# Accumulating the last product of a quad on the bank of the fifth, and setting the output scalings one step further back

## The chip, the cores and the metric

The kernel runs on one core of one Trainium2 chip. The metric is the device time of one execution in microseconds; a version's time is the median of its runs. The engines are named as in the profile: PE is TensorE (matmuls; PEld its weight loads), DVE is VectorE, ACT is ScalarE, POOL is GpSimd, and SP is SyncE, which issues the DMAs.

## The reference

One layer of a gated mixer over 2048 tokens of width 1024, in float32:

```python
h = rms_norm(x, g_pre) * (1 + scale) + shift          # scale, shift, gate from c
pv, pg, hq, hf, hi, hg, mg_pool, mg_hgrn = split(h @ w_in)
pooled = multiscale_pool(pv) @ pool_w * pool_scale
branch_a = (pooled * silu(pg)) @ w_pool_o
f = lb + (1 - lb) * sigmoid(hf);  k = 1 - f;  q = silu(hq)
o = rms_norm(hgrn2(q, k, hi, log(f)), hgrn_norm_g)    # 8 heads of 128
branch_b = (o * silu(hg)) @ w_hgrn_o
merged = sigmoid(mg_pool) * branch_a + sigmoid(mg_hgrn) * branch_b
x = x + gate * rms_norm(merged @ w_out, g_post)
```

hgrn2 is a gated linear recurrence with a 128x128 state for each head. The norm of its output `o` needs, for each token, the sum of squares over the head's 128 channels.

## The kernel before

The tokens are done in two passes of 1024, each as two tiles of 512 tokens (t = 0 and 1). In a pass, the value projection comes first (`psV`), then the eight heads, then the two branches' output projections (`psA`, `psB`), then the output projection (`psy`, in the second pass `ray` and `rxy`).

**Quads.** In the heads, the input projection is done by `quad` (line 522). A quad multiplies a pair of column blocks of `w_in` with both token tiles, a 2x2 block product, by seven products instead of eight (a Strassen-Winograd scheme). Each of the seven is twelve matmuls of 128x512 by `three` (line 327): four blocks of the inner dimension, and for each high x high, high x low and low x high halves of the numbers; all matmuls are issued by line 325. The seven are called by their right-hand side, in this order: `B11`, `T1`, `T2`, `B21`, `T3`, `B22`, `T4`. They accumulate in PSUM banks from a pool of four (`bank`, line 338): `a` (in the profile `pafq`, `pagp`, `pam`, by the kind of quad), `b` (`pb..`), `e` (`pe..`) and `d` (`pd..`). `B11` starts `a`, which is copied to `b`; `T1` starts `e`, copied to SBUF as `s5` (`c22..` in the profile); `T2` adds to `a`, copied out as `u2` (`c12..`); `B21` adds to `b`, the first output; `T3` adds to `a`; `B22` adds to `e`; `T4` adds to `d`. The copies out of PSUM are on ACT (lines 531, 536 and 549), the additions `tt(s5, a, s5)` and `tt(u2, e, u2)` on DVE (line 443, the helper `tt`). Each head has three quads: fq (forget gate and query), m (the two merge gates) and gp (output gate and a pool block); heads 0 to 6 run them in the order fq, m, gp and head 7 in the order fq, gp, m. That makes 48 quads over both passes. The function `got` passes an output on: to a sigmoid on ACT and, for all but the m quads and the forget gate, a multiplication on DVE.

**Steps.** The recurrence of a head (`hgrn`, line 575, one generator for each t) is interleaved with the quads: six times in a quad, and once after it, `tick` advances every active generator by one `yield`. The recurrence of head h starts after its fq quad. Its score matmuls (`psa`) use GAP = 5 steps between levels; DVE puts the scores into a triangle (`PT`, lines 625 and 631) and multiplies K and Q by decays; ACT copies blocks of Q into `X` (lines 658, 661 and 691). In its 25th step, which falls after the fourth product of the next head's second quad, PE makes the output `po`, ACT squares it and sums (`junk`, line 740), POOL turns the sums `ss` into reciprocal roots (line 741, and line 443 with `pow`). In the step after, ACT scales the output by `ss` into `on` (line 746, four for each t). Two steps later PE transposes it (`pot`, line 751), DVE multiplies it by the gate (line 753), and `two_out` splits it into high and low parts and stores both by two DMAs on SP (`Gd`).

**Order.** The source gives the order of the steps, but the order of the instructions in an engine's queue is planned when the program is built: among the instructions that are expected to be ready, the older goes first, and a tile gets its buffer from its pool when one is free. Most tiles of 128x512 share one pool of 76 buffers (`utile`). Weights are read four products ahead (`take`, `prep`), split into high and low parts by ACT and DVE (`whl`, line 173), and in the second pass read back ready split.

Of the kernel before, what the change touches and what calls it, by code (L numbers as in the profile page):

```python
# [70 lines left out]
def tile_block(ctx: ExitStack, tc: tile.TileContext, x, c, w_ada, b_ada, g_pre, g_post, w_in,  # L71
# [3 lines left out]
    V, A, G, PE, SP = nc.vector, nc.scalar, nc.gpsimd, nc.tensor, nc.sync  # L75
# [16 lines left out]
    def utile(name, dt=F32):  # L92
        return up.tile([P, T], dt, tag="u", name=name)
# [219 lines left out]
    def take(look=LOOK):  # L313
        if outs:
            store("out", *outs.pop(0))
        i = state["use"]
        state["use"] = i + 1
        while len(ready) < i + look and more():
            prep()
        w = ready[i]  # L320
        ready[i] = None
        return w[:, 0:T], w[:, T:2 * T]
# [4 lines left out]
    def three(ps, w, rhs, start, stop):  # L327

        hi, lo = w
        n = len(rhs)  # L330
        for k in range(n):
            wh, wl = hi[:, k * P:(k + 1) * P], lo[:, k * P:(k + 1) * P]
            rh, rl = rhs[k]
            mm(ps, wh, rh, start and k == 0, False)
            mm(ps, wh, rl, False, False)
            mm(ps, wl, rh, False, stop and k == n - 1)

    def bank(name):
        return pj.tile([P, T], F32, tag="pj", name=name)
# [96 lines left out]
    def v2(ap, n):  # L436
        return ap.rearrange("p (a b) -> p a b", b=n)
# [4 lines left out]
    def tt(o, a, b, op=MUL, e=None):  # L442
        return (e or V).tensor_tensor(o, a, b, op=op)  # L443
# [78 lines left out]
    def quad(name, cx, got, tick):  # L522

        mv = cx["mv"]

        def prod(ps, nm, start):
            three(ps, take(), [mv[nm, i] for i in range(4)], start, True)

        def snap(ps, nm):
            o = utile(f"{nm}{name}")  # L530
            A.copy(o, ps)
            return o

        a, b = bank("pa" + name), bank("pb" + name)
        prod(a, "B11", True)
        A.copy(b, a)
        e = bank("pe" + name)
        prod(e, "T1", True)
        s5 = snap(e, "c22")
        tick()  # L540
        prod(a, "T2", False)
        u2 = snap(a, "c12")
        tick()
        prod(b, "B21", False)
        got(0, 0, b)
        tick()
        d = bank("pd" + name)
        prod(a, "T3", False)
        A.copy(d, a)
        tt(s5, a, s5, op=ADD)  # L550
        got(1, 1, s5)
        tick()
        prod(e, "B22", False)
        tt(u2, e, u2, op=ADD)
        got(0, 1, u2)
        tick()
        prod(d, "T4", False)
        got(1, 0, d)
        tick()


# [13 lines left out]
    def hgrn(p, h, t, cx):  # L575
# [13 lines left out]
        for hh in (1, 2, 4, 8, 16, 32, 64):  # L589
            w = T // (2 * hh)  # L590
            a = v2(Tb[hh], 2)
# [129 lines left out]
        pd = px.tile([P, NT, P], F32, tag="px", name="pd" + n)  # L721
# [18 lines left out]
            A.activation(junk[:, 0:P], po[:, cc, :], AF.Square, accum_out=ss[:, cc:cc + 1])  # L740
        G.tensor_scalar(ss, ss, 1.0 / P, EPS, op0=MUL, op1=ADD)
        tt(ss, ss, mh[:, 0:NT], op=ALU.pow, e=G)
        yield
        on = utile("on" + n)
        for cc in range(NT):
# [394 lines left out]
    def tick():  # L1140
        for g in list(active):
            try:
                next(g)
            except StopIteration:
                active.remove(g)
# [38 lines left out]
    for p in range(NPASS):  # L1184
# [65 lines left out]
        for h in range(NH):  # L1250
# [19 lines left out]
            def tick_in():  # L1270
                htick()
                once(steps)

            quad("fq" + n, cx, fq, htick)
            active.extend(hgrn(p, h, t, cx) for t in range(2))
            htick()
            for i, kind in enumerate(KINDS[h == NH - 1]):
                if kind == "gp":
                    quad("gp" + n, cx, gp, htick)
                else:  # L1280
                    if h == NH - 1:
                        steps += [lambda: None] * 2
                        steps += [lambda g=g: two_in("P", p, g, cx) for g in range(NG - 1)]
                    quad("m" + n, cx, lambda row, t, u: m_got(p, h, row, t, u, cx), tick_in)
                htick()
# [63 lines left out]
```

## Time and profile before

| | |
|---|---|
| time before, median of 3 runs | 1829.64 us (1827.5 to 1830.42) |
| the profiled execution, its own time | 1831.51 us |
| its span, first to last instruction | 1829.7 us |
| mean granted TensorE clock | 0.996 |
| 140 to 1045 us, from the first quads to those of the second pass | PE busy 891.34 of 905.00 us |
| second pass up to the end of the heads, 1045 to 1600 us | PE busy 550.39 of 555.00 us |

A line of the waits gives who waited, for whom, the microseconds in total, how many times, and the longest. A line of a timeline gives the start and the duration in microseconds, engine, line, operation, output<-inputs, shapes, count, and in brackets the idle time before it with what ended it. A line of the chain of waits gives start, duration and what the chain consists of there. A line for a tile gives minimum, median and maximum in nanoseconds.

### The profile page before, as it was taken

How to read it: one execution, taken by the hardware profiler on the slowest of the kernel's cores; microseconds unless marked ns; L12 is line 12 of the kernel's file. 1: busy time of each engine (PE TensorE's matmuls, PEld its weight loads, DVE VectorE, ACT ScalarE, POOL GpSimd, SP SyncE). 2: the span in 40 equal slices, each digit the busy share in tenths (PEclk: the TensorE clock that was granted, in tenths of full speed). 3: DMA queues.
4: the chain of work that ended last, by engine and by line, in shares of the span. 5: the costliest groups of instructions: out<-in, count | busy, mean ns of one | idle time of the engine just before them, and what ended most of it. 6: DMA issues, size and time to landing. Idle time of an engine off the chain costs nothing.

```text
span 1829.7 us, 32049 instructions
## 1 busy us (share of the span) xinstructions
PE 1772.8 (97%) x12005; PEld 1449.7 (79%) x12005; DVE 1148.9 (63%) x2460; ACT 826.9 (45%) x1939; POOL 77.6 (4%) x136
## 2 busy tenths in 40 slices
PE   5899999999999999999999999999999999999997
PEld 4788878788788787887788878888788788888885
DVE  7577887787888884565443266566566555623446
ACT  4655656556666572223322345455455354310032
POOL 1100000000000100000000000000000000000001
PEclk9999999999999999999999999999999999999998
DMA  8698676777767669987887776876876755695457
GB/s 301 207 321 289 219 271 231 253 253 242 259 236 255 238 222 320 353 304 258 303 293 255 267 256 208 288 259 212 285 238 215 237 179 189 202 348 190 137 208 275
DMA packets 255540, 460.98 MB, mean 252 GB/s; under 512 B 20077, under 2 KB 129306, under 8 KB 255386
## 3 DMA queue, kind: packets, MB, share of 16 engines
q1 hardware_dynamic: 255386, 458.95, 73.1%
q8 instruction: 94, 1.54, 0.3%
q14 instruction: 60, 0.49, 0.1%
HBM read 271.70 MB, written 187.17 MB: 251 GB/s over the span
## 4 chain that ended last, share of the span: by engine, by line
PE 79%; ACT 5%; DMA 4%; DVE 4%; POOL 2%; issue 2%; SPq 0%; POOLq 0%; DVEq 0%; ACTq 0%
PE psB L325 9%; PE psV L325 8%; PE pagp L325 7%; PE pafq L325 7%; PE pam L325 5%; PE pefq L325 5%; PE psA L325 4%; PE pegp L325 4%; PE psy L325 3%; PE pem L325 3%; PE psa L325 3%; PE pbfq L325 2%; PE pdfq L325 2%; PE pdm L325 2%; PE pbm L325 2%; PE pbgp L325 2%
## 5 line engine op out<-in xcount | busy, mean ns | idle before, releaser
L173 DVE TENSOR_TENSOR whl<-wr,whl 128x512 fp32r<-128x512 f32 x210 | 144.1, 690 | 85.7 <-ACT whl L173 84.4
L173 ACT CAST whl<-wr 128x512 fp32r<-128x512 f32 x210 | 130.0, 620 | 127.7 <-PE psB L325 26.5
L325 PE MATMUL psV<-whl,hB 128*128 128x512 f32 x512 | 162.6, 400 | 1.4 <-ACT V L840 1.4
L325 PE MATMUL psB<-Gh,whl 128*128 128x512 f32 x512 | 158.6, 390 | 0.0
L325 PEld LDWEIGHTS psV<-whl,hB 128*128 128x128 f32 x512 | 97.7, 193 | 21.5 <-ACT V L840 1.7
L631 DVE COPY_PREDICATED PT<-mask,psa 128x256 f32<-128x256 uint8 x160 | 86.2, 548 | 44.3 <-PE psa L325 44.2
L325 PEld LDWEIGHTS psB<-Gh,whl 128*128 128x128 f32 x512 | 96.1, 188 | 20.4 <-issue 0.5
L325 PE MATMUL psV<-whl,lB 128*128 128x512 f32 x256 | 101.2, 397 | 0.0
L325 PE MATMUL psB<-Gl,whl 128*128 128x512 f32 x256 | 100.0, 391 | 0.0
L325 PE MATMUL pam<-hT,whl 128*128 128x512 f32 x256 | 87.4, 402 | 0.0
L325 PE MATMUL pagp<-hT,whl 128*128 128x512 f32 x256 | 86.2, 397 | 0.0
L325 PE MATMUL psA<-Ph,whl 128*128 128x512 f32 x256 | 82.6, 397 | 3.4 <-DMA Ph<-Pd 1.7
L325 PE MATMUL pafq<-hT,whl 128*128 128x512 f32 x256 | 84.0, 389 | 0.0
L443 DVE TENSOR_TENSOR K<-K,TT 128x256 f32<-128x256 f32 x192 | 81.4, 425 | 0.7 <-PE psa L325 0.7
L325 PE MATMUL psy<-whl,mgh 128*128 128x512 f32 x256 | 80.6, 395 | 0.7 <-DVE y L443 0.7
L325 PEld LDWEIGHTS psa<-X,K 128*32 128x32 f32 x2816 | 50.0, 110 | 30.0 <-issue 19.2
L325 PE MATMUL psa<-X,K 128*32 128x48 f32 (+2 forms) x2816 | 60.7, 208 | 2.7 <-DVE PT L625 2.7
L443 DVE TENSOR_TENSOR sm<-psB,sm 128x512 f32<-128x512 f32 x32 | 22.0, 688 | 63.8 <-PE psB L325 62.4
L625 DVE COPY_PREDICATED PT<-mask,psa 128x256 f32<-128x256 uint8 (+1 forms) x96 | 52.0, 542 | 12.0 <-PE psa L325 11.9
L325 PEld LDWEIGHTS psA<-Ph,whl 128*128 128x128 f32 x256 | 47.6, 188 | 15.0 <-DMA Ph<-Pd 3.5
L325 PEld LDWEIGHTS psV<-whl,lB 128*128 128x128 f32 x256 | 49.1, 192 | 10.5
L325 PEld LDWEIGHTS pagp<-hT,whl 128*128 128x128 f32 x256 | 48.0, 188 | 10.9 <-issue 0.2
(437 smaller groups left out, 4532.2 us busy)
## 6 DMA issues: line engine op xcount, KB each, us to landing
wr<-in_w_in_dram SPq DMA_DIRECT2D x122, 256.0 KB, 4.7
whl<-scr_y SPq DMA_DIRECT2D x44, 512.0 KB, 4.7
sm<-Sd SPq DMA_DIRECT2D x64, 256.0 KB, 4.6
whl<-scr_v SPq DMA_DIRECT2D x32, 512.0 KB, 4.2
scr_y<-rfy SPq DMA_DIRECT2D x56, 256.0 KB, 3.2
wa<-in_w_ada_dram SPq DMA_DIRECT2D x32, 256.0 KB, 5.4
x<-in_x_dram SPq DMA_DIRECT2D x32, 256.0 KB, 5.4
Vd<-V SPq DMA_DIRECT2D x32, 256.0 KB, 2.4
```

Of the source, the lines that this page charges most:

```text
L173: return A.copy(hi, src32), V.tensor_tensor(lo, src32, hi.bitcast(F32), op=SUB)
L325: PE.matmul(o, lhsT=l, rhs=r, start=start, stop=stop, skip_group_check=True)
L443: return (e or V).tensor_tensor(o, a, b, op=op)
L625: V.copy_predicated(dst.rearrange("p (c a) b -> p c a b", c=NT), m.unsqueeze(1).broadcast_to(shp), src.unsqueeze(2).broadcast_to(shp))
L631: V.copy_predicated(dst.rearrange("p (c q) a b -> p c q a b", c=NT), m, src.rearrange("p c (a b) -> p c a b", b=b).unsqueeze(2) .broadcast ...
```

## The change

`T4` no longer has a bank of its own. It adds to `a`, after `tt(s5, a, s5)` has read from it what `T3` completed, and the last output is read from `a`. The bank `d` and its copy go, so a quad takes three banks of the pool in place of four. In `hgrn`, a second `yield` stands between the sums of squares and the scalings, so that the scalings and everything behind them in that generator come one step later.

```diff
@@ quad @@
         prod(b, "B21", False)
         got(0, 0, b)
         tick()
-        d = bank("pd" + name)
         prod(a, "T3", False)
-        A.copy(d, a)
         tt(s5, a, s5, op=ADD)
         got(1, 1, s5)
         tick()
@@ quad @@
         tt(u2, e, u2, op=ADD)
         got(0, 1, u2)
         tick()
-        prod(d, "T4", False)
-        got(1, 0, d)
+        prod(a, "T4", False)
+        got(1, 0, a)
         tick()
@@ hgrn @@
         G.tensor_scalar(ss, ss, 1.0 / P, EPS, op0=MUL, op1=ADD)
         tt(ss, ss, mh[:, 0:NT], op=ALU.pow, e=G)
         yield
+        yield
         on = utile("on" + n)
```

## The prediction

> **What bounds the kernel now.** I read the page first (span, busy shares, the chain by engine), then the waits of TensorE, then the chain of waits inside one of the places they name, then the engines' queues there.
>
> ```profile
> span 1829.7 us, 32049 instructions
> ...
> PE 1772.8 (97%) x12005; PEld 1449.7 (79%) x12005; DVE 1148.9 (63%) x2460; ACT 826.9 (45%) x1939; POOL 77.6 (4%) x136
> ...
> PE 79%; ACT 5%; DMA 4%; DVE 4%; POOL 2%; issue 2%; SPq 0%; POOLq 0%; DVEq 0%; ACTq 0%
> ```
>
> TensorE (PE) is busy for 97% of the span, so a change pays only where PE stands still. But 5% of the chain that ended last lies on ACT and 2% on POOL, which is itself busy for 4%: somewhere PE hangs on them. The waits of PE say where (total us, times, longest):
>
> ```profile
> PE psa L385 <- DVE acc L378: 13.4, 4, 9.3
> PE pdm L325 <- ACT pdm L549: 6.9, 12, 0.9
> ...
> PE psa L325 <- DVE PT L625: 2.7, 3, 1.4
> ```
>
> The first is the start of the kernel, which the change does not touch. The second is the line that the change deletes: the last product of an m quad (`T4`, into `pdm`) waits for the copy on line 549, in 12 of the 16 m quads. The fq and gp quads do not appear: there the copy is always done in time. The twelve fit the source: the squares of a head are taken during the next head's second quad, after its fourth product. That is an m quad for heads 1 to 6, six times in each pass; head 0 has no such work, and head 7 runs gp second. The chain of waits in one of them (start, us, what):
>
> ```profile
> 235.34 1.08 POOL ss L443
> ...
> 238.47 1.02 POOL ss L443
> ...
> 239.52 1.14 ACT on L746 x4
> 240.66 0.29 ACT X L658
> 240.96 0.50 ACT pdm L549
> 241.45 0.04 issue
> 241.50 3.04 PE pdm L325 x12
> ```
>
> POOL raises the sums of squares to a power (1.0 us each); ACT's scalings (`on`, line 746) stand in ACT's queue ahead of the copy and wait for that; the copy comes last, and PE after it.
>
> **The change part by part.** *What the twelve waits cost.*
>
> ```profile
> 238.16 0.39 PE L325 MATMUL pem<-hB,whl 128*128 128x512 f32 x1
> ...
> 240.65 0.39 PE L325 MATMUL pem<-hB,whl 128*128 128x512 f32 x1
> 241.50 0.50 PE L325 MATMUL pdm<-hT,whl 128*128 128x512 f32 x1 [0.46 <-ACT pdm L549]
> 241.83 0.40 PE L325 MATMUL pdm<-lT,whl 128*128 128x512 f32 x1
> ```
>
> These are the first and last matmul of the sixth product, then the first two of the last. The pitch is (240.65 - 238.16) / 11 = 0.23 us. `T4` starts 0.85 us after its predecessor, not 0.23: 0.62 lost, and the step after it is 0.33, another 0.10. So 0.72 us are lost where 0.46 are idle: 0.26 beyond the idle time. For all twelve: 6.9 + 12 x 0.26 = 10.0 us, and since PE runs back to back afterwards, nearly all of it reaches the end. That is the whole gain to be had from the copy's going.
>
> *What takes the copy's place.* `T4` now adds to the bank `a` that the addition `tt(s5, a, s5)` on DVE reads, and must wait for that read. The order in the trace is not the source's: each engine's queue was planned ahead, older instructions first among those expected to be ready. So the question is where `c22m`, that addition, stands in DVE's queue.
>
> ```profile
> 238.69 0.43 DVE L443 TENSOR_TENSOR sq<-X,TT 128x256 f32<-128x256 f32 x1
> 240.99 0.42 DVE L443 TENSOR_TENSOR sq<-sq,TT 128x256 f32<-128x256 f32 x1 [1.87 <-ACT X L658]
> 241.45 0.42 DVE L443 TENSOR_TENSOR X<-sq,TT 128x256 f32<-128x256 f32 x1
> 241.79 0.69 DVE L443 TENSOR_TENSOR c22m<-pam,c22m 128x512 f32<-128x512 f32 x1
> ```
>
> The two operations ahead of `c22m` belong to a later step than it, so by plan it was not yet ready. Why not, when the fifth product (`T3`) is over once the sixth has begun at 238.16? The copy reads the same bank first:
>
> ```profile
> L549 ACT COPY pdm<-pam x16: 570/612/616, 167.2 to 1591.5; 128x512 f32<-128x512 f32 x16
> ...
> DVE c22fq L443 <- ACT pdfq L549: 13.6, 13, 1.4
> ```
>
> In 13 of 16 fq quads DVE stands idle until the copy has ended and only then adds, though both read the same finished bank: the two reads run one after the other. Without the copy the addition is ready some 0.6 us sooner by plan. Does that lift it over the two others? ACT's queue bounds when the plan had the fifth product end:
>
> ```profile
> 240.53 0.42 ACT L658 COPY X<-sq 128x256 f32<-128x256 f32 x1
> 240.83 0.61 ACT L549 COPY pdm<-pam 128x512 f32<-128x512 f32 x1
> ...
> 241.86 0.43 ACT L661 COPY X<-sq 128x256 f32<-128x256 f32 x1
> ```
>
> Line 658's copy is younger in the source than the bank copy and yet goes first, so by plan the product ended after it was issued. Line 661's, which needs the DVE operation fed by 658, goes later, so the product ended before that operation had run. The end lies in a stretch of about 0.3 us of ACT plus 0.35 of DVE. In its first half DVE is still free and takes `c22m` first; in its second half `c22m` follows one operation. The second pass is alike:
>
> ```profile
> 1139.78 0.43 DVE L443 TENSOR_TENSOR X<-sq,TT 128x256 f32<-128x256 f32 x1
> 1141.62 0.42 DVE L443 TENSOR_TENSOR sq<-sq,TT 128x256 f32<-128x256 f32 x1 [1.41 <-ACT X L691]
> 1141.96 0.42 DVE L443 TENSOR_TENSOR sq<-X,TT 128x256 f32<-128x256 f32 x1
> 1142.41 0.69 DVE L443 TENSOR_TENSOR c22m<-pam,c22m 128x512 f32<-128x512 f32 x1
> ...
> 1143.02 0.42 DVE L443 TENSOR_TENSOR X<-sq,TT 128x256 f32<-128x256 f32 x1
> ```
>
> Here `c22m` overtakes the younger operation at 1143.02 which could have run before it. It was ready by plan at about the end of the one at 1141.96. Less the copy's 0.6, that is when the one at 1141.62 was issued, or before. I take it that `c22m` moves ahead of the operations that wait for ACT. It then runs at about 239.1 to 239.8 in the first case, in DVE's idle 1.87 us, against 240.88 when `T4` is due (240.65 + 0.23): 1.1 us in hand. In the second it ends by 1140.9, 1.5 us before the copy did, where no wait of the twelve was over 0.9. So the term is -10.0 us; the other end is the first rival.
>
> *The other 36 quads* have no wait now. `T4` stays covered by the sixth product as long as the addition ends in time. The latest I found:
>
> ```profile
> 262.83 0.69 DVE L443 TENSOR_TENSOR c22gp<-pagp,c22gp 128x512 f32<-128x512 f32 x1
> ...
> 263.06 0.39 PE L325 MATMUL pdgp<-hT,whl 128*128 128x512 f32 x1
> ```
>
> It ends 0.46 us after `T4` started. One or two such cases: +0.5 us, at most 1.
>
> *The bank* `a` is now held until the last output is read. The next quad's first copy may need that bank only after a product of 12 matmuls; the reader it waits for is short:
>
> ```profile
> L443 DVE TENSOR_TENSOR sq<-pdfq,sq x16: 690/692/693, 153.2 to 1549.8; 128x512 f32<-128x512 f32 x16
> ...
> 245.41 2.75 PE pagp L325 x12
> ```
>
> A sigmoid and this multiplication, some 1.4 us, against 2.75: nothing. Three banks a quad out of four leave one spare; the cost would be the difference if readers fell behind by more than 1.4 us. ACT loses 48 copies (x 0.5 = 24 us), but apart from those twelve waits PE hangs on no ACT copy here: nothing.
>
> *The scalings.* One more empty step moves 8 scalings on ACT, then 8 transposes on PE, two multiplications, the splits and four stores on SP by one step. The transposes stay right after `T4`, since no product lies between the two steps; the stores are read back only after all heads. In an m quad no new buffer of the common pool is asked for between the old place and the new, and nothing older is ready for ACT until the fifth product ends. So I expect the same place in ACT's queue, and the wait for POOL to stay:
>
> ```profile
> ACT on L746 <- POOL ss L443: 27.3, 26, 1.4
> ```
>
> It may move in head 7:
>
> ```profile
> 673.50 0.63 ACT L803 ACTIVATE sgg<-c22gp 128x512 f32<-128x512 f32 x1 [0.19 <-DVE c22gp L443]
> 674.04 2.16 ACT L746 ACTIVATE on<-po,ss 128x128 f32<-128x128 f32 x8
> ```
>
> The scalings already stand behind the output before them, which asks for a buffer; they would go behind the next output, some 2.5 us later, and PE can run a product first. Between 0 and +1 us for each of two; I take 0. Should the scalings move in the m quads too, ACT and DVE are free sooner and the term of 10.0 stays as it is.
>
> Sum: -10.0 + 0.5 = -9.5 us. The profiled execution took 1831.5 us (span 1829.7 and 1.8 around it), so 1822.0 for it; it lies 1.9 above the median of 1829.6, which gives 1820.1.
>
> **The rivals.** *First, slower: the addition stays behind the operations that wait for ACT.* Then `T4` waits for the end of `c22m` (241.79 + 0.69 = 242.48) where it waited for the copy's (240.83 + 0.61 = 241.44): +1.04 us. In the second pass the copy ended about when `c22m` starts, 1142.41, and +0.69 follows. Together 6 x 1.04 + 6 x 0.69 = +10.4 us, with the 0.5 of the gp quads +10.9: 1840.5. For it: that is today's order. Against it: today's order comes from the copy. It decides from the point where `c22m` ends more than 0.6 us after its slot.
> [...]
>
> *Second, no change: half and half.* If `c22m` comes after one operation (240.99, the next starts 0.34 later), it ends at 241.33 + 0.69 = 242.02, 0.58 after the copy's end. First in one pass and second in the other: -6 x 0.72 + 6 x 0.58 + 0.5 = -0.3 us: 1829.3.
>
> *Third, no change: the scalings go so late that the transposes wait.* Eight take 2.16 us (row above). If they start only when `T4` is nearly done, the transposes can begin on the first four, and PE waits for the other half: 12 x 1.08 = 13.0 against the 10.0 gained, with the 0.5 +3.5 us: 1833.1.
>
> **How the numbers follow.** The forecast has 0.58: the argument on the order rests on two bounds that agree, but on no row that shows it. The first rival has 0.20, the second 0.14, the third 0.08. About 0.2%, 3.7 us, is what a measurement can tell here. Faster 0.58, same 0.22, slower 0.20. Low end: 1829.6 - 10.0 - 2.7 (the `psa` waits for DVE, which is relieved too) = 1816.9, so 1816. High end: the cases of no change, the dearer at 1833.1, so 1834; the slower rival, 0.20, is left out.
>
> **What would show it.** Right: no row of PE `pam` waiting for `c22m`; `c22m` starting within 1.2 us of the fifth product's end in the twelve m quads; ACT with 48 copies fewer; `on` still waiting for POOL. Wrong: PE waits of 1 us or more on `c22m` (first rival), waits on some and not on others (second), PE `pot` waiting for `on` (third). If no such wait is there and the time has not fallen, PE lost it elsewhere, and I have missed what.

## The result and the profile after

The changed kernel took 1817.22 us (median of 7 runs, 1815.48 to 1823.29) against 1829.64 (7 runs, 1826.39 to 1832.3): a ratio of 0.9936, interval 0.9925 to 0.9947, so 12.4 us less, 9.7 to 13.7 by the interval. Forecast were 9.5 us. In a later comparison, on another chip, the same change gave 1818.95 against 1830.35, ratio 0.9936 [0.9924, 0.9948]. The profiled execution took 1819.84 us.

The page of the changed kernel: span, busy time, and the chain by engine.

```profile
span 1818.1 us, 32014 instructions
...
PE 1769.1 (97%) x12005; PEld 1449.7 (80%) x12005; DVE 1148.2 (63%) x2460; ACT 799.7 (44%) x1891; POOL 77.3 (4%) x136
...
PE 86%; DMA 5%; DVE 2%; ACT 1%; issue 1%; POOL 1%; SPq 0%; POOLq 0%; DVEq 0%; ACTq 0%
```

ACT has 48 instructions fewer and lost 27 us of work, which is not why the kernel is faster (the experiments show it). What matters is the last row: ACT and POOL, 7% of the chain before, are 2% now.

TensorE's waits (us in total, times, longest) of the changed kernel:

```profile
PE psa L385 <- DVE acc L378: 13.0, 4, 9.7
...
PE pam L325 <- DVE c22m L443: 1.2, 1, 1.2
...
PE pagp L325 <- ACT PV L762: 0.7, 1, 0.7
...
PE pagp L325 <- DMA whl<-scr_('gp', 1)_4_2641: 0.4, 1, 0.4
PE pagp L325 <- DMA whl<-scr_('gp', 2)_4_3467: 0.3, 1, 0.3
PE pot L750 <- ACT on L745: 0.3, 1, 0.3
PE pagp L325 <- DMA whl<-scr_('gp', 3)_4_4315: 0.3, 1, 0.3
```

The row of 6.9 us on the copy has gone with the copy. In its place stands one wait of 1.2 us for the addition `c22m`, not twelve. The row `psa <- DVE PT` of 2.7 us has gone as well, which the sum had not counted. New are small waits in the gp quads, and one of 0.3 us for the scalings' output `on`.

The DVE timeline of the quad whose chain the prediction followed (before at 235 to 242 us, here some 3 us earlier), then the products of the same stretch on PE:

```profile
236.46 0.42 DVE L443 TENSOR_TENSOR sq<-X,TT 128x256 f32<-128x256 f32 x1
236.80 0.68 DVE L443 TENSOR_TENSOR c22m<-pam,c22m 128x512 f32<-128x512 f32 x1
...
239.89 0.42 DVE L443 TENSOR_TENSOR sq<-sq,TT 128x256 f32<-128x256 f32 x1
```

```profile
238.43 0.39 PE L325 MATMUL pem<-hB,whl 128*128 128x512 f32 x1
238.66 0.39 PE L325 MATMUL pam<-hT,whl 128*128 128x512 f32 x1
238.88 0.39 PE L325 MATMUL pam<-lT,whl 128*128 128x512 f32 x1
```

`c22m` now runs ahead of the operation at 239.89 (`sq<-sq`), behind which it stood before, and is over at 237.48. `T4` starts at 238.66, one pitch of 0.23 us after its predecessor and 1.2 us after the addition it depends on.

By stage (starts of the first and last matmul of a kind, from the rows of the tiles; the same rows of the other kernels give the table's other lines):

```profile
L325 PE MATMUL pafq<-hB,whl x128: 387/389/504, 131.1 to 1515.8; 128*128 128x512 f32 x128
L325 PE MATMUL psA<-Ph,whl x256: 388/389/628, 689.5 to 1640.8; 128*128 128x512 f32 x128
L325 PE MATMUL psV<-whl,hB x512: 387/389/775, 24.3 to 1020.8; 128*128 128x512 f32 x171
```

| us | up to the first fq product | first pass, to the first `psA` | to the last `psV` | second pass, to its last fq product | to the end |
|---|---|---|---|---|---|
| before | 133.4 | 565.7 | 333.5 | 497.1 | 300.0 |
| the change | 131.1 | 558.4 | 331.3 | 495.0 | 302.3 |
| the change, other chip | 130.8 | 558.4 | 332.7 | 495.0 | 300.7 |
| second `yield` alone | 130.9 | 566.1 | 331.7 | 499.0 | 301.2 |
| copy gone alone | 130.4 | 557.6 | 330.1 | 494.8 | 301.8 |
| copy kept, but ahead of the scalings | 130.4 | 557.9 | 333.6 | 492.1 | 300.8 |
| copy gone, scalings behind the sigmoid | 130.9 | 557.6 | 332.3 | 491.1 | 301.0 |

The edit touches only the second and the fourth column: -7.3 and -2.1 us, together -9.4. The others lie up to 3.5 us apart between single executions of these kernels; the 2.3 us of the first column are of this kind, for the kernel with the `yield` alone starts as early as the change. The two passes do not gain alike: the first gains more than its half of the forecast, the second less.

### The profile page after: what moved, and what is told of

Read it like the earlier page. It is cut to its first block, busy times and chain, and to the rows that moved or that the text cites. A ratio compares the mean times of both kernels' runs of the same rounds, so it can differ in the third digit from the quotient of the medians.

```text
span 1818.1 us, 32014 instructions
## 1 busy us (share of the span) xinstructions
PE 1769.1 (97%) x12005; PEld 1449.7 (80%) x12005; DVE 1148.2 (63%) x2460; ACT 799.7 (44%) x1891; POOL 77.3 (4%) x136
## 4 chain that ended last, share of the span: by engine, by line
PE 86%; DMA 5%; DVE 2%; ACT 1%; issue 1%; POOL 1%; SPq 0%; POOLq 0%; DVEq 0%; ACTq 0%
PE pafq L325 9%; PE psB L325 9%; PE pam L325 9%; PE pagp L325 8%; PE psV L325 8%; PE pefq L325 5%; PE pegp L325 5%; PE pem L325 4%; PE psA L325 4%; PE psa L325 3%; PE po L325 3%; PE psy L325 3%; PE pbfq L325 2%; PE pbm L325 2%; PE pbgp L325 2%; PE pd L325 1%
## 5 line engine op out<-in xcount | busy, mean ns | idle before, releaser
L325 PE MATMUL pam<-hT,whl 128*128 128x512 f32 x384 | 129.7, 398 | 1.2 <-DVE c22m L443 1.2
L325 PE MATMUL pagp<-hT,whl 128*128 128x512 f32 x384 | 128.7, 396 | 1.6 <-ACT PV L762 0.7
L325 PE MATMUL pafq<-hT,whl 128*128 128x512 f32 x384 | 126.1, 389 | 0.0
L325 PEld LDWEIGHTS pagp<-hT,whl 128*128 128x128 f32 x384 | 72.1, 188 | 18.9 <-issue 2.1
L325 PEld LDWEIGHTS pam<-hT,whl 128*128 128x128 f32 x384 | 72.1, 188 | 17.1 <-DVE c22m L443 1.6
L325 PEld LDWEIGHTS pafq<-hT,whl 128*128 128x128 f32 x384 | 72.1, 188 | 15.0
L325 PE MATMUL pagp<-lT,whl 128*128 128x512 f32 x192 | 75.0, 391 | 0.0
L325 PE MATMUL pam<-lT,whl 128*128 128x512 f32 x192 | 74.9, 390 | 0.0
L325 PE MATMUL pafq<-lT,whl 128*128 128x512 f32 x192 | 74.7, 389 | 0.0
```

Source lines behind the costliest of these rows:

```text
L325: PE.matmul(o, lhsT=l, rhs=r, start=start, stop=stop, skip_group_check=True)
```

## The experiments

The theory: the twelve waits came from the order in ACT's queue, where the copy stood behind scalings that wait for POOL; without the copy `T4` waits for an addition that the sixth product covers. Rivals: ACT was simply too full; the gain comes from the moved scalings; the cover does not matter.

**The change in halves.** First the copy and its bank gone with one `yield` as before, then the second `yield` alone.

> Only the first half of the change: the last product adds to bank a, no copy; the scalings keep their step. My theory (the gain is the end of the twelve waits of the last product for the copy, and the extra step changes nothing in the m quads): 1816 to 1820 us, that is within 3 us of the whole change (1817.2), with no more than two waits of PE pam for c22m, and the wait of on for POOL at about 27 us. Rival (the extra step is what frees ACT, and without it c22m stays behind the operations that wait for ACT): 1825 to 1841 us, with waits of PE pam for c22m of 1 us or more in most m quads.

```diff
-        d = bank("pd" + name)
         prod(a, "T3", False)
-        A.copy(d, a)
...
-        prod(d, "T4", False)
-        got(1, 0, d)
+        prod(a, "T4", False)
+        got(1, 0, a)
```

> Only the second half of the change: the scalings one step later, the copy and its bank kept. My theory: the place of the scalings in ACT's queue moves in head 7 alone, so the twelve waits of pdm for the copy stay (6.9 us idle) and the time is that of before, 1828 to 1831 us. Rival (the step matters): the waits go or shrink to half and the time falls by 4 to 10 us, to 1820 to 1826 us.

```diff
         yield
+        yield
         on = utile("on" + n)
```

The copy gone alone: 1819.38 us, ratio 0.9942 [0.9927, 0.9956], with one wait for `c22m`, of 1.2 us, as in the change. The `yield` alone: 1831.42, 0.4 above the expected range, 1.0008 [0.9999, 1.0016]. TensorE's waits in the latter:

```profile
PE pdm L325 <- ACT pdm L549: 7.3, 12, 0.9
...
PE psa L325 <- DVE PT L625: 2.7, 3, 1.1
```

Both of the old waits are there, twelve and three of them. ACT's waits in it:

```profile
ACT on L747 <- POOL ss L443: 27.3, 26, 1.4
```

That is the figure of before, so the second `yield` seems not to move the scalings in the m quads. The gain is all the copy's.

**The copy kept, but put ahead of the scalings.** Each scaling is queued behind the newest copy of line 549; bank, copy and one `yield` stay.

> The kernel before, copy and bank kept, with one constraint of order: the scalings are queued on ACT behind the newest copy of line 549. My theory (the copy is late because the scalings stand ahead of it and wait for POOL): the copy starts within 0.1 us of the fifth product's end in all m quads, the waits of pdm are gone, and the time falls by about as much as with the change, to 1817 to 1822 us, though all 48 copies are still there. Rival (what counts is ACT's relief of 48 copies, 24 us, or DVE's earlier additions): no more than 3 us, 1826 to 1830 us. A third way: the scalings, now behind the copy, let the transposes wait by 0.5 us or more, which would give part of it back, 1823 to 1826 us.

```diff
-        A.copy(d, a)
+        last["cp"] = A.copy(d, a)
...
-            A.activation(on[:, cc * P:(cc + 1) * P], po[:, cc, :], AF.Copy, scale=ss[:, cc:cc + 1])
+            with after(last.get("cp")):
+                A.activation(on[:, cc * P:(cc + 1) * P], po[:, cc, :], AF.Copy, scale=ss[:, cc:cc + 1])
```

1816.54 us, ratio 0.9931 [0.9918, 0.9945]. Its page and the copies' row:

```profile
PE 1767.0 (97%) x12005; PEld 1449.0 (80%) x12005; DVE 1147.2 (63%) x2460; ACT 824.4 (45%) x1939; POOL 77.3 (4%) x136
```

```profile
L549 ACT COPY pdm<-pam x16: 570/570/581, 164.3 to 1575.8; 128x512 f32<-128x512 f32 x16
```

All copies are made and ACT is as busy as before (824.4 us against 826.9), yet the whole gain is there and the wait `pdm <- ACT pdm` is gone. So ACT's load did not matter; the order did. The expectation missed in two details: the time is 0.5 us under its range, and only in ten of the 16 m quads does ACT stand idle for the fifth product just ahead of the copy (17.7 us in all); in the other six the copy does not follow the product in this way, and is early enough all the same.

**POOL's power left out.** The line that raises the sums of squares to a power is left out, once before the change and once after it, so the scalings find their factor at once (the outputs are not normalized then).

> The kernel before without POOL's power (left out: the sums of squares are scaled, but not raised to -1/2), so that the scalings wait 1 us less for POOL, twice in each group; nothing else is changed. My theory (POOL's time ahead of the copy makes the twelve waits): the copy is at most 1.2 us after the fifth product, well inside the sixth's 2.7 us, the waits of pdm are gone and the time is 1817 to 1822 us. Rival (the waits come from ACT's load as such): the waits stay within 2 us of 6.9 and the time above 1826 us.

> The whole change without POOL's power (left out: the sums of squares are scaled, but not raised to -1/2). My theory: after the change POOL's time matters only in the one m quad whose last product still waits for c22m (1.2 us idle), so 0 to 2 us less than the changed kernel, 1814 to 1818 us. Rival (the waits of ACT for POOL, 27 us, still cost PE time somewhere else): 5 us or more, below 1812 us.

```diff
-        tt(ss, ss, mh[:, 0:NT], op=ALU.pow, e=G)
```

Before without the power: 1815.84 us, ratio 0.992 [0.9907, 0.9933]. The change without it: 1816.91, 0.9923 [0.9908, 0.9938]. Without POOL's 1.0 us ahead of the scalings, the change is worth nothing: the two ratios agree within their intervals. Before without the power came out 1.2 us under the range expected for it. The copy itself costs nothing that can be measured here; what was paid for was POOL's time, handed on by the order of ACT's queue to a copy that had nothing to do with it.

**The cover taken away.** The product `B22` is done before `T3`, so that `T4` follows `T3` directly; the weights are read in the new order. Everything is still computed.

> The whole change, with the sixth product (B22) done before the fifth (T3), so that no product stands between the addition that reads bank a and the last product that adds to it; the weights are taken in the same new order. My theory (the change costs nothing only because a product of 2.7 us covers the addition): the last product waits for DVE in most of the 48 quads, about 0.04 + 0.69 us for the addition and 0.3 for the lost overlap, 1.0 us each and more where DVE is behind, less where other matmuls of the step fill the gap: plus 20 to 50 us, 1837 to 1867 us. Rival (PE finds other work, or the addition is soon enough without cover): within 5 us of the changed kernel, 1813 to 1822 us.

```diff
-                return [lambda i=i: again((key, i), f"{base + i}") for i in range(7)]
+                return [lambda i=i: again((key, i), f"{base + i}") for i in (0, 1, 2, 3, 5, 4, 6)]
...
+        prod(e, "B22", False)
+        tt(u2, e, u2, op=ADD)
+        got(0, 1, u2)
+        tick()
         prod(a, "T3", False)
         tt(s5, a, s5, op=ADD)
         got(1, 1, s5)
         tick()
-        prod(e, "B22", False)
-        tt(u2, e, u2, op=ADD)
-        got(0, 1, u2)
-        tick()
         prod(a, "T4", False)
```

1871.34 us, ratio 1.0226 [1.0208, 1.0244]: 54 us above the change. TensorE's waits, then one of them on PE:

```profile
PE pam L325 <- DVE c22m L443: 25.5, 15, 2.8
...
PE pagp L325 <- DVE c22gp L443: 2.4, 7, 0.4
```

```profile
249.63 0.50 PE L325 MATMUL pam<-hT,whl 128*128 128x512 f32 x1 [2.64 <-DVE c22m L443]
249.97 0.40 PE L325 MATMUL pam<-lT,whl 128*128 128x512 f32 x1
250.20 1.01 PE L325 MATMUL pam<-hT,whl 128*128 128x512 f32 x2
251.01 0.63 PE L325 MATMUL pam<-lT,whl 128*128 128x512 f32 x1
...
253.57 0.44 PE L325 MATMUL pam<-lT,whl 128*128 128x512 f32 x1
```

More than the 20 to 50 us that were expected, though only 22 of the 48 quads wait, not most of them. It is the wait on `c22m` that the first rival names, 1.7 us on average and 2.8 at most. It shows the dependence the change creates: what keeps it free in the change is the other product of 2.75 us between. The idle time is 25.5 + 2.4 = 27.9 us, and 22 restarts at the prediction's 0.26 add 5.7. A further part is the matmuls after the wait: the last row is the eleventh of the twelve, and from the first to it there are 3.94 us where ten pitches of 0.23 would be 2.3, so some 1.6 us, 0.1 of it in the restart already. Six of the waits have such a slow stretch and a seventh has one of twice the length (the last section shows both): about 8 x 1.5 = 12. Of the 54 that leaves some 8, which I have not traced to their places.

**The scalings later still.** In the change, each scaling is queued behind the newest sigmoid of an m quad, so that in most heads it comes after POOL is done, but late.

> The whole change, with one constraint of order: the scalings are queued on ACT behind the newest sigmoid of an m quad, so that in the m quads they really stand two steps behind the squares, after the sixth product's output. The third rival of the prediction: the transposes wait for them, up to 1.1 us in each of twelve quads, 1825 to 1832 us. My theory: ACT has room, the transposes wait 0 to 0.5 us in each, 1816 to 1823 us, and the wait of on for POOL (27.3 us in before) falls to under 5 us without any gain from it.

```diff
-        A.activation(s, u, AF.Sigmoid)
+        last["cp"] = A.activation(s, u, AF.Sigmoid)
```

The scalings stand under `with after(last.get("cp"))` as above. It took 1819.79 us, ratio 0.9944 [0.9931, 0.9957]: no better than the change. TensorE waits for the transposes' inputs, in the matmuls and, more often, in their weight loads:

```profile
PE pot L751 <- ACT on L746: 1.4, 4, 0.4
```

```profile
PEld pot L751 <- ACT on L746: 9.0, 24, 0.8
```

The third rival's mechanism is real, and from the first fq product to the last `psV` it takes 892.9 us where the change takes 889.7, and 891.1 on the other chip. Its size is not what the rival gave it: the longest wait on PE is 0.4 us where the rival had 1.08.

**The scalings behind the right sigmoid.** The copy gone, one `yield`, and the scalings behind the sigmoid of the fifth product's output: late enough for POOL, early enough for the transposes.

> The copy gone as in the change, the scalings without the extra step, but queued on ACT behind the sigmoid of the fifth product's output in the m quads, so that nothing on ACT waits for POOL ahead of what DVE needs for c22m. My theory: the one remaining wait for c22m (1.2 us idle, 1.4 lost) goes, the head 7 delay of the transposes too, and the time is 1 to 3 us under the copy's going alone: 1814 to 1818 us. Rival (the transposes after the last product now wait for the scalings): 1820 us or more.

```diff
-        A.activation(s, u, AF.Sigmoid)
+        it = A.activation(s, u, AF.Sigmoid)
+        if (row, t) == (1, 1):
+            last["cp"] = it
```

The scalings stand under `with after(last.get("cp"))` here too. It took 1816.32 us, ratio 0.9921 [0.991, 0.9933], and ACT hardly waits for POOL any more:

```profile
ACT on L745 <- POOL ss L443: 0.7, 2, 0.4
```

It was run again beside the change on one chip:

> The change as it is, on the same chip as the next run, to set the two side by side. 1816 to 1819 us, ratio to before 0.992 to 0.995.

> The copy gone, the scalings one step behind the squares and queued behind the sigmoid of the fifth product's output in the m quads, once more beside the change. My theory: it saves the change's one wait for c22m and the late transposes of head 7, 1 to 3 us, so 1814 to 1817 us; rival: what looked better was the chip, and the two agree within 1 us.

The change 1818.95 us, ratio 0.9936 [0.9924, 0.9948]; this version 1816.68, 0.9926 [0.9911, 0.9942]. Its medians are the lower both times, by 0.9 us (against the change on another chip) and 2.3 us, but the intervals overlap: it is as good as the change, and whether it is better is not settled by the times. The profile says where it would be: the waits for `c22m` and in the gp quads are gone, and the second pass takes 491.1 us, in the second run 491.5, in place of 495.0.

## Why the prediction came out as it did

**The twelve waits of the copy (-10.0 us): right.** All twelve waits for the copy are gone, and in eleven of the places nothing has come in their stead; the mechanism, a copy behind scalings that wait for POOL, is shown by the copy put first (gain without removing it) and by the power left out (gain gone).

**`c22m` moves ahead of the operations that wait for ACT: right in eleven of twelve.** In these it starts 0.7 to 1.2 us after the fifth product; in four quads of the second pass it still follows an operation that waits for ACT, but by 0.2 to 0.3 us only, and `T4` is covered. The exception is the m quad of head 5 in the second pass, where it starts 3.1 us after the product. The changed kernel's DVE, ACT and PE there:

```profile
1415.84 0.42 DVE L443 TENSOR_TENSOR sq<-sq,TT 128x256 f32<-128x256 f32 x1 [2.37 <-ACT X L689]
1416.18 0.68 DVE L443 TENSOR_TENSOR c22m<-pam,c22m 128x512 f32<-128x512 f32 x1
```

```profile
1414.37 1.14 ACT L745 ACTIVATE on<-po,ss 128x128 f32<-128x128 f32 x4 [1.35 <-POOL ss L443]
1415.38 0.42 ACT L689 COPY X<-sq 128x256 f32<-128x256 f32 x1
```

```profile
1415.37 0.39 PE L325 MATMUL pem<-hB,whl 128*128 128x512 f32 x1
1416.92 0.50 PE L325 MATMUL pam<-hT,whl 128*128 128x512 f32 x1 [1.16 <-DVE c22m L443]
```

Read from the bottom: `T4` waits for `c22m`, which stands behind an operation that waits for ACT's copy, which stands behind a scaling that waits for POOL. That is the first rival, in one quad of twelve, at 1.2 us.

**The term that was mis-sized: the `psa` waits.** The prediction gave 2.7 us for TensorE's waits for DVE at the scores only as its low end and counted nothing in the sum. They went, all three. One of them before, then the same place after, on PE:

```profile
269.31 0.39 PE L325 MATMUL pafq<-hB,whl 128*128 128x512 f32 x1
271.07 0.22 PE L325 MATMUL psa<-X,K 128*32 128x32 f32 x1 [1.37 <-DVE PT L625]
```

```profile
266.32 0.39 PE L325 MATMUL pafq<-hB,whl 128*128 128x512 f32 x1
266.64 0.22 PE L325 MATMUL psa<-X,K 128*32 128x32 f32 x1
```

From the last product's matmul to the scores it was 1.76 us and is 0.32: 1.4 saved. In the other two it was 1.18 and 0.95 and is 0.32 as well. Together that is 2.9, all in the first pass; the 0.26 beyond the idle time does not come on top here. The three vanish in every kernel in which `T4` does not wait for the copy, the one that keeps its copies included, and stay with the `yield` alone. So they do not hang on ACT's load; that they follow from the wait of `T4` fits every run, but was not followed step by step.

The twelve waits were not alike in the two passes. Before, TensorE's waits for the copy in the first pass (130 to 700 us), then in the second (1045 to 1600 us):

```profile
PE pdm L325 <- ACT pdm L549: 3.1, 6, 0.6
```

```profile
PE pdm L325 <- ACT pdm L549: 3.7, 6, 0.9
```

With 0.26 for each wait these are 4.7 and 5.3 of the 10.0. So the first pass: 4.7 and 2.9 make 7.6, against 7.3 measured.

**Where the second pass lost part of its gain.** Of its 5.3 us, head 5's wait takes back 1.2 idle and 0.26, and the four waits in the gp quads, 0.7, 0.4, 0.3 and 0.3 idle, take back 2.7 with their 0.26 each; 1.2 should be left. Measured were 2.1 against before, and 4.0 against the `yield` alone, whose second pass has the six waits of the copy and two in the gp quads: one execution each does not settle it closer. The gp waits the prediction did not have; its +0.5 for the other quads was for another cause, and no wait for `c22gp` appeared.

Head 5's wait hangs on the wait of ACT for POOL, as the rows above show, and without that wait it is gone. Whether the gp waits hang on it too is open. For it: where the scalings wait 27.3 us for POOL (the change in both runs, the copy gone alone) the second pass takes 494.8 to 495.0; where they wait 0.7 us (the copy put first, the two with the scalings behind a sigmoid) or at most 6.2 (the two without the power) it takes 491.1 to 492.5, and there are no gp waits. Against it: the kernel before has the 27.3 and no gp wait, and in the second execution of the change the three for DMA are missing. Of that execution's second pass:

```profile
PE pbfq L325 <- DMA whl<-scr_('fq', 0)_3_1390: 2.0, 1, 2.0
PE pam L325 <- DVE c22m L443: 1.2, 1, 1.2
PE pagp L325 <- ACT PV L762: 0.7, 1, 0.7
```

Its first row is a wait for the weights of a head's first quad, 0.6 us in the first execution; so that both come to 495.0 is chance.

**Bank `a` and ACT's relief (nothing each): right.** No wait for a bank came up, and the kernel that keeps the copies is as fast.

**The scalings: right.** Their wait for POOL is 27.3 us in 26 places, unchanged; in head 7 PE waits once, 0.3 us, for `on`.

**The sum.** In the two stages that the edit touches, -9.4 us against -9.5: that closeness is partly luck. The forecast had no 2.9 for the `psa` waits, and it allowed 0.5 for losses in other quads, where the second pass lost 4.1 by other waits; the two nearly cancel. The spans of the two profiled executions differ by 11.6; the 2.2 between lie in stages that the edit leaves alone, where single executions differ by as much. The medians fell by 12.4, and what is beyond that is not explained.

## What to carry to other kernels

A wait on a copy is not a reason to make the copy cheaper: look at what stands ahead of it in its engine's queue, and at what that waits for; here the whole gain came with all 48 copies kept. The spare PSUM bank could be given up with a product that does not need it between the read and the next accumulation (2.75 us against 0.69 for the read); without that product between them the same edit cost 54 us more. And when one of TensorE's waits goes, look at its other waits as well: here three that the forecast had counted at nothing, 2.9 us, went along with it.

## What the hardware showed beside that

With the cover gone, TensorE did not only stand still: after a wait of 1.8 to 2.8 us the matmuls came every 0.43 us instead of 0.23, for about 3 us, in one case for nearly 6. Windows of that kernel: from the wait shown above on, then inside that slow stretch, then inside the longest one (us, PE, PEld, DVE, ACT and POOL busy, granted clock, DMA share, GB/s):

```profile
249.00:258.00 9.00, 8.37 (x32) 6.47 (x33) 5.75 (x10) 3.47 (x8) 0.00 (x0) 0.81 0.81 289
258.00:270.00 12.00, 12.00 (x110) 9.74 (x109) 10.02 (x21) 4.80 (x10) 0.00 (x0) 1.00 0.76 264
...
250.30:253.60 3.30, 3.30 (x10) 2.52 (x9) 1.95 (x4) 0.00 (x0) 0.00 (x0) 0.50 1.02 348
629.20:635.90 6.70, 6.04 (x14) 4.78 (x15) 2.53 (x5) 1.15 (x3) 0.00 (x0) 0.50 0.75 264
```

The granted clock is 0.81 over the nine microseconds and 1.00 over the twelve after; inside the slow stretches it is 0.50: over 3.3 us after 250 us, and over the 6.7 us around the longest. Seven of the eight waits of 1.8 us and more for `c22m` were followed by such a stretch; the eighth (2.62 us) and the seven shorter ones (0.2 to 1.1 us) were not. An idle time of 1.8 us was enough, and one of 2.62 us was not; what else decides it, no run here shows.
